# Second attention: a diagonal of softmax factors in place of the identity under three of four turned heads, and three buffers for turned tiles

## The chip, the cores and the metric

One core of a Trainium2 chip runs the whole program. The metric is its execution time in microseconds; times of the whole kernel are medians of runs. The profile is of one execution and is read by engine: PE (TensorE, matrix products and transposes through the array), DVE (VectorE), ACT (ScalarE), POOL (GpSimd) and SP, which issues most transfers.

## What is computed

The reference runs two transformer blocks one after the other on 512 tokens. The change lies in the attention of the second block. Each of its 16 query heads (two groups of eight, one key and value head for each group) attends in three ways: over 31 compressed blocks, over selected blocks (here all causal ones, since at most 8 of 16 picks exist) and over a window of 512. The three results are mixed by gates of each token and head:

```
s_c = einsum(qb, k_cmp) * scale;  p_c = masked_softmax(s_c, ...);  o_c = einsum(p_c, v_cmp)
s_s = einsum(qb, k_sel) * scale;  p_s = masked_softmax(s_s, ...);  o_s = einsum(p_s, v_sel)
s_w = einsum(qb, kwb)   * scale;  p_w = masked_softmax(s_w, ...);  o_w = einsum(p_w, vwb)
o = gb[..., 0:1] * o_c + gb[..., 1:2] * o_s + gb[..., 2:3] * o_w
```

So a row of exponentials must be multiplied by one factor: its gate divided by its sum.

## The kernel before

The tokens lie in four tiles of 128. For each of the two groups `g`, `queries(g)` makes the rotated queries, and then `attend(i, g, c, ...)` is called for each query tile `i` (0 to 3) and each `c` (0, 1), which stands for four heads: 16 calls. In a call, n = (i + 1) x 128 keys are seen.

In a call, PE forms scores of 128 queries by n keys for each of the four heads `a` and for two branches `br` (selected, window) into a PSUM bank (`s` or `sw`; L1439 and L1440, two products each); those with the compressed keys go along (`pc`). DVE adds the mask and takes the row's extreme (L1469). ACT takes the exponential and the row sum into `sm` (L1472). The compressed part `cs` goes through DVE, POOL and ACT by itself (L1476 to L1485). When all sums stand, DVE inverts them (L1482) and multiplies them by the gates (L1484); `sm[:, 1 + br, a]` is then the factor of a head and branch, one number for each query, and queries lie on partitions.

Then the exponentials are multiplied by their factors in place: heads 0 to 2 on DVE (L1493, six instructions of 128 x n), head 3 on ACT (L1491, two). After that PE turns them, so that keys lie on partitions: for each branch and each key tile `j` four transposes against the identity `ident` fill one PSUM bank `tp` (L1505), DVE (where j % 3 is 1) or ACT copies it to an SBUF tile `pT` of 128 x 512 (L1507), and two products with the values add it to the output bank `o` (L1510). Ahead of them the compressed part is turned (L1496), copied (L1498) and multiplied (L1500). At the end `split` makes the high and low part of `o` (`ynh`, `ynl`).

All operands of these transposes and of L1500 and L1510 are plain fp32. There are two `tp` banks, four `pT` buffers, three `s` banks, one `o` bank and 12 buffers for the exponentials. A scheduler lays out the order of the instructions on each engine when the program is built; it mixes in other products, those of the next group's queries and, in the second group, of the pooled branch (`mm`, L256, and `yp`, L1552). The attention runs from about 1905 to 2105 us of the span; behind it comes a long stretch of gated projections.

Of the kernel before, what the change touches and what calls it, by code (L numbers as in the profile page):

```python
# [9 lines left out]
F32 = mybir.dt.float32  # L10
# [3 lines left out]
AF = mybir.ActivationFunctionType  # L14
OP = mybir.AluOpType
AX = mybir.AxisListType

P = 128
T = 512
# [147 lines left out]
def build(tc, A, OUT):  # L167
    nc = tc.nc
    es = ExitStack()
    V, S, G, TE = nc.vector, nc.scalar, nc.gpsimd, nc.tensor  # L170
# [23 lines left out]
    def tpps(name="tp"):  # L194
        return bank(tp_tag[0], name)
# [7 lines left out]
    ident = cst[:, C_ID:C_ID + P]  # L203
# [35 lines left out]
    def wfm(name, c, kt=KD, width=P, c0=0):  # L239

        n = kt * width
        return kview(weights(A[name][c][:, c0:c0 + n], n, 2), kt, width)
# [218 lines left out]
    def mtwo(name="m2"):  # L461
        return tp.tile([P, L], F32, name=name, tag="m2", bufs=9)
# [66 lines left out]
    x = mtwo()  # L529
# [5 lines left out]
    pt = tpps(name="kpp")  # L535
    for t, t0, m in toks(L):
        TE.transpose(pt[:m, t * 32:(t + 1) * 32], x[:32, t0:t0 + m], ident[:32, :32])
    for t0, t1, m in ((0, NT, P), (NT, NT + 1, M)):
        h = t1 - t0
        pv = pt[:m, t0 * 32:t1 * 32].rearrange("p (t d) -> p t d", t=h)  # L540
        x = mtwo()
# [90 lines left out]
    def fm_pieces(w, pieces):  # L632

        x = two(t2)
        for a, b in pieces:
            ps = mmps()
            fm(ps[:, :b - a], w, hn, 0, a, b - a)
            S.copy(x[:, a:b], ps[:, :b - a])
        return x
# [110 lines left out]
    for h in range(8):  # L750
        x = fm_pieces(wfm("w_rv", h), PIECES)
        pt = tpps()
# [5 lines left out]
        pt = tpps()  # L758
# [102 lines left out]
    for c in range(KD):  # L861
        x = gate("w_za", c, two(t2)[:, :T])
# [45 lines left out]
    sts = ExitStack()  # L908
# [430 lines left out]
    for br in range(2):  # L1339
# [3 lines left out]
        r = rope_fm(ps)  # L1343
        o = (KS, KW)[br]
        for g in range(2):
            a, b = slice(g * 64, g * 64 + 64), slice(64 - g * 64, 128 - g * 64)
# [7 lines left out]
        x = two(t2)[:, :T]  # L1354
        S.copy(x, ps)
        pt = tpps()
# [10 lines left out]
    x = two(t2)[:48, :T]  # L1367
    S.activation(x, ps[:48], AF.Tanh, scale=0.5)
    V.tensor_scalar(x, x, 1.0, 0.5, op0=OP.add, op1=OP.mult)
    pt = tpps()  # L1370
# [11 lines left out]
    pt = tpps()  # L1382
# [12 lines left out]
    pt = tpps()  # L1395
# [11 lines left out]
    ap_ = pool("attn2", stack=sta)  # L1407
# [18 lines left out]
    def attend(i, g, c, Q, yh, yl):  # L1426

        n, t0 = (i + 1) * P, i * P
        cs = ap_.tile([P, 4, 32], F32, name="cs", bufs=2)
        mx = ap_.tile([P, 4, 2], F32, name="mx2", bufs=2)  # L1430
        sm = ap_.tile([P, 3, 4], F32, name="sm2", bufs=2)
        mc = ap_.tile([P, 4], F32, name="mc", bufs=2)
        mask = cst[:, C_MASK + (3 - i) * P:C_MASK + 512]
        cmask = cst2[:, K_CMP + i * 64:K_CMP + i * 64 + 32]
        sts = []

        def score(out, a, k0, m):
            q = Q[c][:, a, t0:t0 + P]
            TE.matmul(out, q, KH[:, g, k0:k0 + m], start=True, stop=False)  # L1439
            TE.matmul(out, q, KL[:, g, k0:k0 + m], start=False, stop=True)  # L1440

        if i == NT - 1:
            pc = bank("s", "pc")
            for a in range(4):
                score(pc[:, a * 32:a * 32 + 32], a, KC, 32)
            V.tensor_tensor(cs, pc[:, :P].rearrange("p (a k) -> p a k", a=4),
                            cmask[:, None, :].to_broadcast([P, 4, 32]), op=OP.add)
        for a in range(4):
            ps = bank("s", "s")
            if i == 0:  # L1450
                score(ps[:, :KS + P], a, K0, KS + P)
                src = (ps[:, KS:KS + P], ps[:, :P])
                pc = ps[:, KC:KC + 32]
            else:
                k0 = KS if i == NT - 1 else KC
                score(ps[:, :KS + n - k0], a, k0, KS + n - k0)
                pw = bank("s", "sw")
                score(pw[:, :n], a, KW, n)
                src = (ps[:, KS - k0:KS - k0 + n], pw[:, :n])
                pc = ps[:, :32]  # L1460
            if i < NT - 1:
                V.tensor_tensor(cs[:, a], pc, cmask, op=OP.add)
            s2 = []
            for br in range(2):
                if i < 2 and br:
                    s = s[:, n:]
                else:
                    s = ap_.tile([P, T], F32, name="s2", bufs=12)
                V.tensor_tensor_reduce(out=s[:, :n], in0=src[br], in1=mask, scale=-SC, scalar=3e38,  # L1469
                                       op0=OP.add, op1=OP.min, accum_out=mx[:, a, br:br + 1])  # L1470
                s2.append(s)
                S.activation(s[:, :n], s[:, :n], AF.Exp, scale=-1.0, bias=mx[:, a, br:br + 1],  # L1472
                             accum_out=sm[:, 1 + br, a:a + 1])
            sts.append(s2)

        V.tensor_reduce(mc, cs, axis=AX.X, op=OP.max)  # L1476
        G.tensor_tensor(cs, cs, mc[:, :, None].to_broadcast([P, 4, 32]), op=OP.subtract)
        S.activation(cs, cs, AF.Exp, scale=SC)
        V.tensor_reduce(sm[:, 0], cs, axis=AX.X, op=OP.add)
        G.tensor_tensor(cs, cs, cst2[:, None, K_CMP + i * 64 + 32:K_CMP + i * 64 + 64].to_broadcast([P, 4, 32]), op=OP.mult)  # L1480

        V.reciprocal(sm, sm)  # L1482
        h0 = 8 * g + 4 * c
        V.tensor_tensor(sm, sm, gv[:, i, :, h0:h0 + 4], op=OP.mult)  # L1484
        G.tensor_tensor(cs, cs, sm[:, 0, :, None].to_broadcast([P, 4, 32]), op=OP.mult)  # L1485
        for a in range(4):
            for br in range(2):
                s = sts[a][br][:, :n]
                r = sm[:, 1 + br, a:a + 1]
                if a == 3:  # L1490
                    S.activation(s, s, AF.Copy, scale=r)  # L1491
                else:
                    V.tensor_scalar(s, s, r, None, op0=OP.mult)  # L1493
        po = bank("o", "o")
        pt = tpps()
        TE.transpose(pt[:, :P], cs.rearrange("p a k -> p (a k)"), ident)  # L1496
        pT = ap_.tile([P, T], F32, name="pT", bufs=4)
        V.tensor_copy(pT[:, :P], pt[:, :P])  # L1498
        for j in range(2):
            TE.matmul(po[:, j * P:(j + 1) * P], vcb[:, g, j], pT[:, :P], start=j == 0, stop=False, skip_group_check=True)  # L1500
        for br in range(2):
            for j in range(i + 1):
                pt = tpps()
                for x, a in enumerate((0, 2, 1, 3)):
                    TE.transpose(pt[:, x * P:(x + 1) * P], sts[a][br][:, j * P:(j + 1) * P], ident)  # L1505
                pT = ap_.tile([P, T], F32, name="pT", bufs=4)
                (V.tensor_copy if j % 3 == 1 else S.copy)(pT, pt)  # L1507
                last = br == 1 and j == i
                for b in range(2):
                    TE.matmul(po[b * 64:b * 64 + 64, :2 * P], vt[:, j, br, g], pT[:, b * 256:b * 256 + 256],  # L1510
                              start=False, stop=last, skip_group_check=True)
        pv = po[:, :2 * P].rearrange("p (j t) -> p j t", j=2)
        split(pv, yh[:, 2 * c:2 * c + 2, t0:t0 + P], yl[:, 2 * c:2 * c + 2, t0:t0 + P])
# [46 lines left out]
    for c in range(KD):  # L1560
        y = gate("w_gm", KD + c, two(t2)[:, :T])
        gated("w_pn", c, ysl, KD, y)
        x = gate("w_gm", c, two(t2)[:, :T])
# [88 lines left out]
```

## Time and profile before

| what | us |
|---|---|
| median of 3 runs | 2685.57 (2683.2 to 2687.15) |
| the profiled execution | 2681.29 |
| its span | 2679.5 |
| PE busy in the span | 2585.8 |
| DVE busy in the span | 1702.9 |
| ACT busy in the span | 1146.1 |
| POOL busy in the span | 926.6 |

The span goes from the first to the last instruction of the profiled execution. Busy times of PE are modelled from pipelined instructions and overlap, so that a busy PE need not be working at its full pace; the pace is read from how many instructions of a kind pass in a given time in the chain of waits. In the trace an instruction keeps the line of the code that made it, and one matrix product in the code may be several instructions.

### The profile page before, as it was taken

The numbers are of one execution on the slowest core, as the hardware profiler recorded it, in microseconds if no ns is written. First come the engines' busy times: TensorE is split into PE (matmuls) and PEld (weight loads), VectorE is DVE, ScalarE is ACT, GpSimd is POOL, SyncE is SP. The second block draws the span as 40 slices with busy tenths as digits, with TensorE's granted clock in tenths as the row PEclk, the third lists the DMA queues.
The fourth block names the chain that finished last, engine by engine and source line by source line (L and its number), as shares of the span: only waits on it lengthen the run. The fifth ranks groups of instructions, "written<-read, shape, count | busy, mean of one in ns | idle before, by whom it ended". The sixth has DMA issues, their size and how long they took to land.

```text
span 2679.5 us, 37137 instructions
## 1 busy us (share of the span) xinstructions
PE 2585.8 (97%) x13809; PEld 2225.1 (83%) x13809; DVE 1702.9 (64%) x3399; ACT 1146.1 (43%) x2097; POOL 926.6 (35%) x590
## 2 busy tenths in 40 slices
PE   8899999999899999999999999999999999899998
PEld 7768778899899988888888888887666788787887
DVE  5772442246998992898989888866778412534333
ACT  5552342244577663333333333334667422422322
POOL 2122122325344342565555555522222233211112
PEclk9999999999999999999999999998999999999999
DMA  3322223323356568999999999963110122222221
GB/s 129 100 69 68 67 75 122 119 84 118 103 174 195 168 199 290 331 368 400 402 408 370 339 351 333 337 203 108 53 43 25 60 95 96 109 94 95 94 95 63
DMA packets 177957, 465.80 MB, mean 174 GB/s; under 512 B 15856, under 2 KB 78960, under 8 KB 171120
## 3 DMA queue, kind: packets, MB, share of 16 engines
q1 hardware_dynamic: 136736, 322.84, 34.7%
q0 software_dynamic: 36864, 134.23, 13.6%
q10 hardware_dynamic: 4176, 6.36, 0.8%
q8 instruction: 108, 1.77, 0.3%
q14 instruction: 73, 0.60, 0.1%
HBM read 421.17 MB, written 37.42 MB: 171 GB/s over the span
## 4 chain that ended last, share of the span: by engine, by line
PE 78%; DVE 14%; ACT 2%; DMA 2%; issue 2%; POOL 1%; ACTq 1%; SPq 0%; DVEq 0%; POOLq 0%
PE mm L256 36%; PE py L1182 19%; PE pu L256 13%; DVE oh L1093 3%; PE o L1510 2%; PE tp L1505 1%; DMA t<-t 1%; PE mm L1101 1%; DVE xn L350 1%; DVE oh L1065 1%; DVE oh L1068 1%; DVE oh L1096 1%; PE s L699 1%; DVE ef L1070 1%; DMA wr<-in_u_T_dram 1%
## 5 line engine op out<-in xcount | busy, mean ns | idle before, releaser
L211 POOL TENSOR_TENSOR wl<-wr,wh 128x1024 fp32r<-128x1024 f32 (+1 forms) x142 | 349.9, 2465 | 764.5 <-ACT wh L210 329.5
L210 ACT CAST wh<-wr 128x1024 fp32r<-128x1024 f32 (+2 forms) x271 | 273.4, 1010 | 311.2 <-PE mm L256 203.4
L256 PE MATMUL pu<-xf,wh 128*128 128x384 f32 x2048 | 392.3, 343 | 10.3 <-ACT wh L210 5.8
L256 PEld LDWEIGHTS pu<-xf,wh 128*128 128x128 f32 x2048 | 362.0, 190 | 16.3 <-ACT wh L210 6.2
L211 DVE TENSOR_TENSOR wl<-wr,wh 128x1024 fp32r<-128x1024 f32 (+2 forms) x129 | 152.0, 1179 | 184.0 <-ACT wh L210 112.2
L974 POOL DMA_INDIRECT row<-in_v_rows_dram,eg x128 | 195.7, 1529 | 163.7 <-DVE yg L989 136.9
L974 POOL DMA_INDIRECT row<-in_u_rows_dram,eg x128 | 187.8, 1467 | 176.2 <-DVE row L979 155.1
L256 PE MATMUL pu<-xf,wl 128*128 128x384 f32 x1024 | 202.4, 339 | 2.6 <-POOL wl L211 2.6
L1169 ACT CAST ah<-act 128x384 fp32r<-128x384 f32 x128 | 65.8, 514 | 324.0 <-DVE act L1166 302.2
L1182 PE MATMUL py<-vl,ah 128*128 128x512 f32 x768 | 195.8, 389 | 0.1
L1182 PE MATMUL py<-vh,ah 128*128 128x512 f32 x768 | 195.7, 389 | 0.0
L1182 PE MATMUL py<-vh,al 128*128 128x512 f32 x768 | 195.6, 389 | 0.0
L256 PEld LDWEIGHTS pu<-xf,wl 128*128 128x128 f32 x1024 | 182.5, 189 | 3.5 <-POOL wl L211 3.5
L1174 DVE TENSOR_TENSOR vl<-vr,vh 128x1024 fp32r<-128x1024 f32 x128 | 156.3, 1221 | 22.3 <-ACT vh L1172 22.3
L1182 PEld LDWEIGHTS py<-vl,ah 128*128 128x128 f32 x768 | 144.0, 188 | 30.6 <-DVE vl L1174 0.7
L1182 PEld LDWEIGHTS py<-vh,al 128*128 128x128 f32 x768 | 144.2, 188 | 30.0
L989 DVE SCALAR_TENSOR_TENSOR yg<-row,ag,yg 128x1024 f32<-128x1024 f32 x127 | 162.9, 1282 | 5.3 <-DMA row<-in_v_rows_dram,eg 2.9
L1182 PEld LDWEIGHTS py<-vh,ah 128*128 128x128 f32 x768 | 143.3, 188 | 25.4
L979 DVE SCALAR_TENSOR_TENSOR row<-row,xg 128x1024 f32<-128x1024 f32 x128 | 152.3, 1221 | 9.9 <-DMA row<-in_u_rows_dram,eg 9.9
L1093 DVE TENSOR_TENSOR oh<-iota,eT 128x1024 f32<-128x1024 f32 x96 | 139.8, 1483 | 14.0 <-PE mm L1101 12.6
L381 DVE TENSOR_TENSOR h<-mm,h 128x512 f32<-128x512 f32 (+1 forms) x54 | 34.1, 632 | 172.6 <-PE mm L256 172.6
L1172 ACT CAST vh<-vr 128x1024 fp32r<-128x1024 f32 x128 | 134.6, 1051 | 19.5 <-PE py L1182 18.7
(468 smaller groups left out, 5103.3 us busy)
## 6 DMA issues: line engine op xcount, KB each, us to landing
wr<-in_u_T_dram SPq DMA_DIRECT2D x128, 512.0 KB
vr<-in_v_rows_dram SPq DMA_DIRECT2D x128, 512.0 KB
wwr<-in_w_f_dram SPq DMA_DIRECT2D x32, 1024.0 KB
gates<-stg SPq DMA_DIRECT2D x24, 1024.0 KB
gin<-gates SPq DMA_DIRECT2D x16, 1536.0 KB
wr<-in_w_gm_dram SPq DMA_DIRECT2D x16, 512.0 KB
ahead<-act SPq DMA_DIRECT2D x41, 192.0 KB
act<-ahead SPq DMA_DIRECT2D x41, 192.0 KB
```

Of the source, the lines that this page charges most:

```text
L210: S.copy(hi, src)
L211: (lo_eng or V).tensor_tensor(lo, src, hi.bitcast(F32), op=OP.subtract)
L256: TE.matmul(out, w[a][k][:, c0:c0 + P], act[b][k][:, t0:t0 + n], start=i == 0 and k == 0, stop=i == 2 and k == kt - 1)
L974: G.indirect_dma_start(out=r, out_offset=None, in_=src, in_offset=bass.IndirectOffsetOnAxis(ap=eg[:, k:k + 1], axis=0))
L979: V.scalar_tensor_tensor(r, r, 1.0, xg, op0=OP.mult, op1=OP.mult, accum_out=ag[:, k:k + 1])
L989: V.scalar_tensor_tensor(yg[0], r, ag[:, k:k + 1], yg[0], op0=OP.mult, op1=OP.add)
L1093: V.tensor_tensor(a1, iota[:, None, None, :].to_broadcast([P, 2, 4, P]), eT[:, :2, b0 + q0:b0 + q0 + 4, None].to_broadcast([P, 2, 4, P]), ...
L1169: S.copy(ah, a)
L1172: S.copy(vh, raw)
L1174: V.tensor_tensor(vl, raw, vh.bitcast(F32), op=OP.subtract)
L1182: TE.matmul(py[2 * t + d], x[:, t * P:(t + 1) * P], w[:, d * 512:(d + 1) * 512], start=e == 0 and i == 0, stop=e == P - 1 and i == 2)
L1510: TE.matmul(po[b * 64:b * 64 + 64, :2 * P], vt[:, j, br, g], pT[:, b * 256:b * 256 + 256], start=False, stop=last, skip_group_check=True)
```

## The change

The multiplications of heads 0 to 2 are gone. Instead DVE makes for each branch a tile `dg` of 128 x 3 x 128 that holds three diagonal matrices: the identity times the factor of head 0, 1 and 2 of each query. Under these heads the transpose against the identity becomes an ordinary product against the diagonal, which turns and scales in one go. Head 3 is still scaled by ACT and turned by a transpose. `dg` has two buffers of 1.5 KB on each partition, one for each branch; `pT` has three buffers in place of four.

```diff
-        for a in range(4):
-            for br in range(2):
-                s = sts[a][br][:, :n]
-                r = sm[:, 1 + br, a:a + 1]
-                if a == 3:
-                    S.activation(s, s, AF.Copy, scale=r)
-                else:
-                    V.tensor_scalar(s, s, r, None, op0=OP.mult)
+        dg = [ap_.tile([P, 3, P], F32, name="dg", bufs=2) for br in range(2)]
+        for br in range(2):
+            V.tensor_tensor(dg[br], ident[:, None, :].to_broadcast([P, 3, P]),
+                            sm[:, 1 + br, :3, None].to_broadcast([P, 3, P]), op=OP.mult)
+            s = sts[3][br][:, :n]
+            S.activation(s, s, AF.Copy, scale=sm[:, 1 + br, 3:4])
...
-        pT = ap_.tile([P, T], F32, name="pT", bufs=4)
+        pT = ap_.tile([P, T], F32, name="pT", bufs=3)
...
                 for x, a in enumerate((0, 2, 1, 3)):
-                    TE.transpose(pt[:, x * P:(x + 1) * P], sts[a][br][:, j * P:(j + 1) * P], ident)
-                pT = ap_.tile([P, T], F32, name="pT", bufs=4)
+                    s = sts[a][br][:, j * P:(j + 1) * P]
+                    if a < 3:
+                        TE.matmul(pt[:, x * P:(x + 1) * P], s, dg[br][:, a], start=True, stop=True)
+                    else:
+                        TE.transpose(pt[:, x * P:(x + 1) * P], s, ident)
+                pT = ap_.tile([P, T], F32, name="pT", bufs=3)
```

The order of the instructions changes with it in the whole second attention. Two places show how, both in the first call with four key tiles of the second group (g = 1, i = 3, c = 0). On DVE before, the factors are followed by a score tile's minimum, by six scalings and by the copy of the turned compressed part:

```order
L1484 TENSOR_TENSOR sm_19029<-sm_19029,gts 128x12
L1469 ISA s_19218,mx_19187<-s,cstt 128x512
L1469 ISA mx_19187 128x1
L1493 TENSOR_SCALAR s_19047<-s_19047,sm_19029 128x512
L1493 TENSOR_SCALAR s_19050<-s_19050,sm_19029 128x512
L1493 TENSOR_SCALAR s_19059<-s_19059,sm_19029 128x512
L1493 TENSOR_SCALAR s_19062<-s_19062,sm_19029 128x512
L1493 TENSOR_SCALAR s_19071<-s_19071,sm_19029 128x512
L1493 TENSOR_SCALAR s_19074<-s_19074,sm_19029 128x512
L1498 COPY pT<-tp 128x128
```

On DVE now (lines behind the change have other numbers: the copy L1498 is L1497):

```order
L1484 TENSOR_TENSOR sm_19001<-sm_19001,gts 128x12
L1469 ISA s_19188,mx_19157<-s,cstt 128x512
L1469 ISA mx_19157 128x1
L1489 TENSOR_TENSOR dg<-cstt,sm_19001 128x384 x2
L1497 COPY pT<-tp 128x128
L1469 ISA s_19191,mx_19157<-sw,cstt 128x512
```

The two builds stand where the six scalings stood. On PE before, the first turned tiles of the same call have products of the pooled branch (L256) between them:

```order
L1505 MATMUL tp<-cstt,s_19047 128x128
L256 MATMUL mm<-h2h,wh 128x512 x6
L1505 MATMUL tp<-cstt,s_19071 128x128
L1505 MATMUL tp<-cstt,s_19059 128x128
L1505 MATMUL tp<-cstt,s_19083 128x128
L256 MATMUL mm<-h2h,wh 128x512 x2
L1500 MATMUL o<-pT,vcb 128x128 x2
L1510 MATMUL o<-pT,vt 64x256 x2
L1505 MATMUL tp<-cstt,s_19047 128x128
```

On PE now (L1506 is the product with the diagonal, L1508 the transpose, L1499 the former L1500, L1513 the former L1510):

```order
L1506 MATMUL tp<-dg,s_19019 128x128
L1506 MATMUL tp<-dg,s_19043 128x128
L1506 MATMUL tp<-dg,s_19031 128x128
L1499 MATMUL o<-pT,vcb 128x128 x2
L1508 MATMUL tp<-cstt,s_19055 128x128
L1506 MATMUL tp<-dg,s_19019 128x128
L1506 MATMUL tp<-dg,s_19043 128x128
```

The turning products now stand in closer rows, and the L256 products that lay between them have moved to other places, many of them behind the call.

## Rows read from the trace of the kernel before

**Rows 1.** The page: busy us, share of the span, instructions.
```profile
PE 2585.8 (97%) x13809; PEld 2225.1 (83%) x13809; DVE 1702.9 (64%) x3399; ACT 1146.1 (43%) x2097; POOL 926.6 (35%) x590
```

**Rows 2.** Busy times by stretch of the span, us: the attention and its four parts.
```profile
core 0: us, PE busy (x) PEld busy (x) DVE busy (x) ACT busy (x) POOL busy (x), PEclk, DMA share, GB/s
1905.00:2105.00 200.00, 190.57 (x1163) 130.66 (x1161) 157.70 (x550) 144.99 (x400) 43.09 (x67) 1.00 0.10 31
1911.00:1944.00 33.00, 29.16 (x186) 19.75 (x184) 29.10 (x135) 28.36 (x94) 6.41 (x13) 1.00 0.05 11
1944.00:2004.00 60.00, 56.94 (x352) 37.25 (x352) 42.86 (x108) 41.16 (x90) 11.95 (x13) 1.00 0.11 35
...
2014.00:2052.00 38.00, 36.42 (x221) 26.32 (x220) 34.64 (x138) 30.89 (x95) 12.68 (x19) 1.00 0.09 31
2052.00:2105.00 53.00, 52.82 (x337) 35.23 (x337) 37.96 (x110) 33.55 (x77) 7.10 (x15) 1.00 0.06 19
```

**Rows 3.** Chain of waits, 1905 to 2110: start us, us, what.
```profile
1949.36 0.59 PE tp L1505 x4
...
2057.35 1.01 PE o L1510 x8
2058.37 1.02 PE tp L1505 x8
...
2067.30 0.58 PE o L1510 x4
...
2079.91 1.39 PE mm L256 x6
...
2082.09 0.45 PE o L1500 x4
```

**Rows 4.** PE by line, 1905 to 2105: count, busy us, mean ns, idle before.
```profile
L1505 PE MATMUL tp<-cstt,s 128*128 128x128 f32 x320 | 51.9, 281 | 2.6 <-DVE s L1493 2.6
L1510 PE MATMUL o<-pT,vt 128*64 128x256 f32 x320 | 48.4, 400 | 0.4 <-DVE pT L1507 0.2
...
L256 PE MATMUL mm<-h2l,wh 128*128 128x512 f32 x64 | 21.0, 413 | 0.0
...
L1500 PE MATMUL o<-pT,vcb 128*128 128x128 f32 x64 | 10.2, 282 | 0.0
```

**Rows 5.** DVE by line and shape, 1905 to 2105: count, busy us, mean ns.
```profile
L1493 DVE TENSOR_SCALAR s<-s,sm 128x512 f32<-128x512 f32 x24 | 10.3, 495 | 0.0
L1493 DVE TENSOR_SCALAR s<-s,sm 128x384 f32<-128x384 f32 x24 | 8.5, 418 | 0.0
...
L1493 DVE TENSOR_SCALAR s<-s,sm 128x256 f32<-128x256 f32 x24 | 7.0, 357 | 0.0
...
L1493 DVE TENSOR_SCALAR s<-s,sm 128x128 f32<-128x128 f32 x24 | 5.6, 298 | 0.1
...
L1537 DVE TENSOR_TENSOR t<-t 128x511 f32<-128x511 f32 x4 | 2.7, 680 | 0.0
...
L1446 DVE TENSOR_TENSOR cs<-pc,cst 128x128 f32<-128x128 f32 x4 | 1.2, 292 | 3.7 <-PE pc L1440 3.7
```

**Rows 6.** Instructions in order of time in a call with four key tiles.
```profile
1989.13 2.55 DVE L1493 TENSOR_SCALAR s<-s,sm 128x512 f32<-128x512 f32 x6
...
1991.60 0.28 DVE L1498 COPY pT<-tp 128x128 f32<-128x128 f32 x1
```

**Rows 7.** Who waited for whom, 1905 to 2110: total us, times, longest us.
```profile
ACT pT L1507 <- PE tp L1505: 24.9, 28, 2.8
...
DVE pT L1507 <- PE tp L1505: 16.2, 16, 5.1
...
PEld o L1510 <- ACT pT L1507: 6.5, 24, 0.8
...
PEld tp L1505 <- DVE s L1493: 4.0, 6, 1.4
...
PE tp L1505 <- DVE s L1493: 2.6, 4, 1.1
```

## Prediction

> **What bounds the kernel now.** I read the page first: TensorE (PE) is busy 97% of the span, VectorE (DVE) 64% [rows 1]. That PE share is modelled, so it does not say how much PE could still take. Second I read the busy times by stretch, around the second attention, 1905 to 2105 us [rows 2]. The 16 calls of attend fall into four stretches: small query tiles of group 0 (i = 0, 1: 33 us), large ones (i = 2, 3: 60 us), and the same of group 1 (38 and 53 us). DVE is busy 88% and 91% in the two small stretches, 71% and 72% in the large ones. The granted clock is 1.00 in all four, so no gain or loss can come from the clock.
>
> How full PE really is comes from the pace of its instructions, read from the chain of waits [rows 3]: eight transposes take 1.02 us and four 0.59, so one more costs (1.02 - 0.59) / 4 = 0.108 us; the products into `o` give (1.01 - 0.58) / 4 = 0.108; four instructions of the 128x128 product at L1500 take 0.45, so 0.11; six 512-wide instructions of L256 take 1.39, so 0.232. The counts of 1905 to 2105 [rows 4] are 320 transposes (L1505), 320 instructions of L1510, 64 of L1500 and 191 of L256 (three rows of 64, 64 and 63). That leaves 1163 - 895 = 268 others, mostly score products of 256 to 512 columns, which I put midway between 0.11 and 0.23, at 0.17. Work: 35 + 35 + 7 + 44 + 46 = 167 us of 200. PE thus waits some 33 us here, and one instruction is 167 / 1163 = 0.143 us of work on average. By that mean the four stretches hold 26.6, 50.3, 31.6 and 48.2 us of PE work, and so 6.4, 9.7, 6.4 and 4.8 us of idle PE. So the small stretches are near DVE's limit, and the large ones near PE's.
>
> **The change part by part.**
>
> *Transposes become products.* Of the four heads three are multiplied by a diagonal. Which heads: 3 of 4 of 320, so 240. What a true product costs here is shown by L1500, which has the same 128x128 fp32 operands: the code issues 32 of them (2 in each of 16 calls) and the trace holds 64 instructions [rows 4], two for each product, at 0.11 us each [rows 3]; a transpose is one instruction of 0.108. So each of the 240 grows from 0.11 to 0.22 us: **240 x 0.11 = +26.4 us of PE work**: 4.0 us in each small stretch (36 products), 9.2 in each large one (84). The second weight load of each product I cost at nothing: L1500 has it too and still goes at 0.11 a piece; uncovered it would be inside that price.
>
> The Trainium skill speaks against this edit: "Perfetto Trace Analysis", section Transposes, asks that a logical transpose be a transpose and not a standard matmul, since transposes skip the arithmetic. By that rule PE work grows, without a figure. In "TensorE: Matmul & The Clock Gate", section Terms, the fp32 transpose mode is called four times faster; by that the added work would be an estimated 79 us instead of 26. The trace disagrees with the factor: two instructions against one, each at the same 0.11 [rows 3, 4].
>
> *The scalings go from DVE.* 96 TENSOR_SCALAR of 10.3 + 8.5 + 7.0 + 5.6 = 31.4 us leave [rows 5]. Instead 32 builds of a 128x384 diagonal come, a two-operand fp32 op that the trace has not at this size. Its neighbours: 0.29 us at 128 elements and 0.68 at 511 [rows 5]; between them 0.29 + 0.39 x 256 / 383 = 0.55 us. I take 0.55 (bounds 0.41, the price of a 128x384 scaling, and 0.68), so 32 x 0.55 = 17.6 us. **DVE is relieved of 13.8 us**, 3.5 in each small stretch (12 x 0.298 + 12 x 0.357 - 8 x 0.55), the other half in the large ones. The bounds give 18.3 and 9.6.
>
> *The hand-over in a call gets shorter.* Before, the six scalings stand in one run ahead of the copy L1498 on DVE, and PE waits for both: at 1989.1 the run takes 2.55 us and only then the copy starts [rows 6]. The new order has two builds there, 1.1 us, and then the copy. PE's own waits for the scalings, though, sum to only 2.6 + 4.0 us [rows 7], since other products fill most of the time. This is what DVE's relief can give at most directly: some 4 of these 6.6 us. It is part of the relief and not added to it.
>
> *A new wait.* The two diagonals are two buffers, so the builds of a call wait until the transposes of the call before are through; behind them on DVE stand the copy L1498, which PE waits for, and the row minima of the next call. In the new order all turning products of a call stand ahead of the next call's first use, so I put this at 0 (bounds 0 and one build in each call, 16 x 0.55 = 9 us). *Three pT buffers in place of four*: three are in flight in the new order (one of the compressed part and two), so 0; at most a wait of one pair of products, 0.43 us, in each call, 7 us. ScalarE (ACT) keeps its 32 scalings of the fourth head.
>
> **The sum.** A stretch takes PE's work and what idle PE is left. I let half of the idle remain, because part of it is waiting for a turned tile to be copied (25 us of ACT and 16 of DVE waiting for transposes, against 6.5 of PE waiting for ACT's copies [rows 7]): while PE does longer products, the copies of the tile before are hidden. The small stretch of group 0 then takes 26.6 + 4.0 + 3.2 = 33.8 us against 33, so +0.8; the large one 50.3 + 9.2 + 4.9 = 64.4 against 60, +4.4; the small one of group 1 31.6 + 4.0 + 3.2 = 38.8 against 38, +0.8; the large one 48.2 + 9.2 + 2.4 = 59.8 against 53, +6.8.
>
> That is +12.8. In the small stretches, where DVE is the later one, I grant half of its 3.5 us twice: -3.5. Sum **+9.3 us**. The profiled execution took 2681.3 us (span 2679.5), 4.3 below the median of 2685.6; so 2690.6 for such an execution, and 2685.6 + 9.3 = **2695 us** as the median. Ends: all idle taken up, 167 + 26.4 = 193.4 of 200, gives -6.6; none taken up, +26.4.
>
> **The rivals.**
>
> *DVE leads all through (faster).* If PE waits because DVE is late everywhere, the stretch follows DVE, and 13.8 us less there come off until PE itself is full. Place: the small stretches and the run of scalings. For it: 88% and 91% busy DVE [rows 2], the 2.55 us run [rows 6]. Against it: PE's 193 us of work set a floor 6.6 us below today's 200, and in the large stretches DVE idles 28%. It decides from the point where less than 0.5 us of idle PE is left. Price: 2685.6 - 6.6 = 2679 us.
>
> *Idle PE takes it all (no change).* Most of the 33 us of waits were for copies and for DVE, and the longer products lie in them. Then +26.4 is met by 20 to 30 us: within 5.4 us of today, about 2686. For it: the waits for copies [rows 7]. Against it: in the large stretches only 14.5 us of idle stand against 18.4 added.
>
> *Full price (slower still).* The idle does not shrink, because the filling products are laid out otherwise and the diagonals' buffers hold DVE: +26.4, 2712 us. For it: of the chain's own time the transposes are a large part already, and PE leads in the large stretches. Against it: DVE's relief and the copies that get hidden.
>
> *Four passes a product.* If a product with the diagonal took the time of four transposes, each would cost three more: 240 x 3 x 0.11 = 79 us, of which some 20 fall into idle PE, so 2685.6 + 59 = 2745. This is the factor of the page named above. Against it stands L1500, which takes two instructions for the same shapes and types [rows 4].
>
> **How the numbers follow.** 0.2% is 5.4 us, about what a measurement of this kernel can tell from no change. Forecast (+5.4 to +17): 0.50. Idle takes it all (within 5.4): 0.24. DVE leads: 0.13. Full price (+17 to +30): 0.10. Four passes: 0.03. So faster 0.13, same 0.24, slower 0.50 + 0.10 + 0.03 = 0.63. The range for 8 in 10 takes the forecast, the no-change case, and the near parts of the two neighbours: 2680 to 2711.
>
> **What would show it.** In the profile after: 560 instructions where 320 turned tiles before (480 with the diagonal, 80 transposes), at 0.11 us each in the chain; 32 builds of 0.41 to 0.68 us; DVE's busy time down by 10 to 18 us; the stretch from the first to the last turned tile about 9 us longer, almost all of it at i = 2 and 3, the small stretches about even; PE's waits for DVE's factors gone. I am wrong if a product with the diagonal takes one instruction, or one of 0.05 us; if the small stretches shorten by more than 3 us each; or if DVE waits for PE before the builds.

## The result and the profile after

The changed kernel is slower: 2713.6 us median (2711.63 to 2716.26, 4 runs) against 2684.78 for the kernel before on the same chip, a ratio of 1.0111 with a 95% interval of 1.0099 to 1.0123. That is **+28.8 us, where +9.3 was forecast**. The direction was right, the size three times too small, and 2713.6 lies above the range (2680 to 2711). The rival "full price" (2712 us), which had a chance of 0.10, has the right number; of its two reasons the runs bear out the filler that is laid out otherwise, but not the buffers of the diagonals.

In the changed kernel the copy L1498 is L1497, the former L1500 is L1499, the copy L1507 is L1510, the products L1510 are L1513, and the builds are L1489. First the busy times of the page of the kernel after (us, share of the span, instructions), beside [rows 1]:

```profile
PE 2623.1 (97%) x14049; PEld 2259.6 (83%) x14049; DVE 1691.2 (62%) x3335; ACT 1148.6 (42%) x2097; POOL 934.9 (34%) x590
```

PE has 240 instructions more, as forecast, and 37.3 us more of (modelled) busy time; DVE has 11.7 us less. The same view by stretch as [rows 2], cut at the calls of the kernel after: the whole attention, then small and large tiles of group 0, small and large tiles of group 1.

```profile
core 0: us, PE busy (x) PEld busy (x) DVE busy (x) ACT busy (x) POOL busy (x), PEclk, DMA share, GB/s
1905.00:2135.00 230.00, 224.42 (x1407) 163.35 (x1407) 146.50 (x487) 147.66 (x401) 46.88 (x67) 0.99 0.09 27
1911.00:1948.00 37.00, 34.70 (x225) 24.42 (x223) 29.58 (x123) 29.76 (x98) 7.09 (x14) 1.00 0.06 14
1948.00:2009.00 61.00, 60.60 (x400) 42.57 (x401) 30.81 (x83) 36.80 (x82) 9.04 (x11) 1.00 0.06 19
2028.00:2063.00 35.00, 34.75 (x232) 26.57 (x233) 30.69 (x118) 28.39 (x88) 9.83 (x16) 1.00 0.09 31
2063.00:2127.00 64.00, 62.15 (x408) 44.47 (x408) 32.21 (x88) 34.62 (x81) 8.33 (x13) 0.97 0.03 9
```

The granted clock is 1.00 in the first three parts and 0.97 in the last (0.83 from 2110 to 2120 us, which is worth 1.7 us of full clock and so little of the 28.8). DVE's share falls from 71 and 72% to 51 and 50% in the large stretches, and PE leads there by a wide margin. The operations themselves are as forecast (line, engine, operation, shapes, count, busy us, mean ns, idle before; answering [rows 4] and [rows 5]):

```profile
L1506 PE MATMUL tp<-dg,s 128*128 128x128 f32 x480 | 73.8, 287 | 0.1
L1508 PE MATMUL tp<-cstt,s 128*128 128x128 f32 x80 | 22.2, 277 | 0.0
L1489 DVE TENSOR_TENSOR dg<-cstt,sm 128x384 f32<-128x384 f32 x32 | 20.1, 663 | 0.2
```

Who waited for whom, 1905 to 2140, in total us, times and longest wait, answers [rows 7]:

```profile
ACT pT L1510 <- PE tp L1508: 37.9, 35, 3.1
DVE pT L1510 <- PE tp L1508: 31.6, 20, 5.8
...
PEld tp L1495 <- POOL cs L1485: 7.7, 10, 2.3
...
PEld o L1513 <- ACT pT L1510: 5.7, 24, 0.4
```

PE's waits for the scalings are gone, and its wait for ACT's copies is a little shorter (5.7 against 6.5). The two engines that copy turned tiles now wait 69.5 us for PE, where it was 41.1. Next to nothing waits on the new builds: PE's load queue waited for one of them 0.3 us, and DVE sat idle 0.2 us ahead of them. PE's wait for the compressed part, whose last step POOL does, has nothing to do with the change and stays (7.7 us above). Before it was:

```profile
PEld tp L1496 <- POOL cs L1485: 8.5, 11, 2.2
```

**Where the 28.8 us lie.** The spans of the two profiled executions are 31.7 us apart (2711.2 and 2679.5); 27.5 of them lie in the attention, as the table shows. The starts of the turned compressed part (L1496, now L1495) mark the calls, and the last products of a group mark its end. Filler is the products of L256, for the next queries and for the pooled branch.

| stretch | before, us | after, us | filler before | filler after |
|---|---|---|---|---|
| small tiles, group 0 | 33.1 | 36.8 | 5 | 5 |
| large tiles, group 0 | 59.1 | 60.7 | 48 | 22 |
| from group 0 to group 1 | 11.1 | 19.3 | 33 | 64 |
| small tiles, group 1 | 37.7 | 34.9 | 45 | 23 |
| large tiles, group 1 | 53.4 | 64.0 | 35 | 25 |
| from the last call to the next product with ynh | 1.9 | 8.1 | 7 | 34 |
| sum | 196.3 | 223.8 | 173 | 173 |

The calls are 13.1 us longer. That this is near the forecast's 9.3 is chance, since it counted no filler as leaving them. The other 14.4 us stand in the two stretches between calls, of which the forecast said nothing: 58 filler instructions have left the calls, and 58 x 0.232 = 13.5 us. The filler's rows alone (windows of L256 only: PE busy us and instructions; a window cut at a whole us can count a few of its neighbour's) show it, first before, then after:

```profile
1944.00:2003.00 59.00, 15.09 (x48) 8.61 (x48) 1.00 0.12 35
2003.00:2014.00 11.00, 8.41 (x33) 5.93 (x33) 1.00 0.26 74
```

```profile
1948.00:2009.00 61.00, 7.06 (x22) 4.30 (x23) 1.00 0.06 19
2009.00:2028.00 19.00, 15.90 (x65) 11.56 (x63) 1.00 0.30 84
```

**How much PE really waited before.** The chain of waits of the kernel before runs for long stretches through PE alone, each piece starting where the last one ends (start us, us, what):

```profile
1950.12 0.58 PE o L1510 x4
1950.71 0.59 PE tp L1505 x4
1951.29 0.18 PE sw L1440
1951.47 0.58 PE o L1510 x4
1952.05 0.59 PE tp L1505 x4
1952.64 0.58 PE o L1510 x4
1953.22 0.21 PE pc L1439
```

There is no wait here, and yet four products into `o` take 0.58 us, and not 4 x 0.108 = 0.43. In the whole attention before, each of the 44 rows of four takes 0.582 us or more (median 0.583) from its start to the next instruction, and each of the 18 rows of eight 1.015: 43.9 us for the 320, where the forecast counted 35. From the last of them to what follows it is 0.309 to 0.310 us, nearly always, whether a turning, a score product or a filler stands next. So 0.15 us is a fixed cost of such a row, not a wait. The same holds for a row of four turnings between such rows (0.59 us). The forecast took the difference of rows of four and of eight as the pace, and called the fixed part idle.

Counted anew, from start to start with every instruction at the pace of its kind (0.109 us for a turning, 0.108 for a product into `o`, 0.23 for 512 columns, and so on), PE stands still for over 0.12 us at 28 places before, 14.0 us in all. After it is 27 places and 10.4 us. Smaller gaps, which are mostly the fixed costs, went from 24.1 to 31.7 us, and work from 158.2 to 181.6 (26 of products, less 2.6 for six products of the pooled branch that moved behind). These sums shift by some us with the paces that are taken, their differences by about 1 us. So the waits shrank by 3.5 us, and the small gaps took 7.6 more. Nor need the 3.5 us be the products' doing: in the kernel with the builds and without the products (below) the waits shrink at least as much, to 9.8 us. And of the 14.0 us, 6.1 stood ahead of the turned compressed part, for which POOL is late, where a longer turning does not reach.

### The profile page after: what moved, and what is told of

Read it like the earlier page. It is cut to its first block, busy times and chain, and to the rows that moved or that the text cites. A ratio compares the mean times of both kernels' runs of the same rounds, so it can differ in the third digit from the quotient of the medians.

```text
span 2711.2 us, 37556 instructions
## 1 busy us (share of the span) xinstructions
PE 2623.1 (97%) x14049; PEld 2259.6 (83%) x14049; DVE 1691.2 (62%) x3335; ACT 1148.6 (42%) x2097; POOL 934.9 (34%) x590
## 5 line engine op out<-in xcount | busy, mean ns | idle before, releaser
L256 PE MATMUL pu<-xf,wh 128*128 128x384 f32 x2048 | 391.0, 342 | 10.3 <-ACT wh L210 5.4
L256 PEld LDWEIGHTS pu<-xf,wh 128*128 128x128 f32 x2048 | 360.9, 190 | 16.5 <-ACT act L961 5.8
L256 PE MATMUL pu<-xf,wl 128*128 128x384 f32 x1024 | 201.2, 338 | 2.6 <-POOL wl L211 2.6
L256 PEld LDWEIGHTS pu<-xf,wl 128*128 128x128 f32 x1024 | 181.4, 188 | 3.5 <-POOL wl L211 3.5
L211 POOL TENSOR_TENSOR wwl<-wwr,wwh 128x2048 fp32r<-128x2048 f32 x11 | 51.7, 4702 | 263.4 <-ACT wwh L210 263.4
```

The source lines that it names most:

```text
L211: (lo_eng or V).tensor_tensor(lo, src, hi.bitcast(F32), op=OP.subtract)
L256: TE.matmul(out, w[a][k][:, c0:c0 + P], act[b][k][:, t0:t0 + n], start=i == 0 and k == 0, stop=i == 2 and k == kt - 1)
```

## The experiments

The first theory: an added turning product is paid in full, since it stands on the chain from turning to copy to product, with PE the latest link. Rivals: the builds or the buffers hold the kernel, the two `tp` banks do, or the order in which filler is laid out.

**The products alone.** The scalings stay, and the three heads are turned by products with the plain identity.

```diff
-                    TE.transpose(pt[:, x * P:(x + 1) * P], s, ident)
+                    if a < 3:
+                        TE.matmul(pt[:, x * P:(x + 1) * P], s, ident, start=True, stop=True)
+                    else:
+                        TE.transpose(pt[:, x * P:(x + 1) * P], s, ident)
```

> The scalings stay on VectorE and pT keeps four buffers, but heads 0 to 2 are turned by an ordinary product against the identity: the 240 longer turnings alone. Full price (a turning product holds up all that follows on TensorE, none of it falls into idle time): +24 to +28 us over the kernel before. Half absorbed, as I forecast: +11 to +15 us. If the +29 of the changed kernel comes from the builds, their two buffers or the third pT buffer: under +10 us.

Measured: 2711.66 us, 1.0105 (1.0086 to 1.0124), +27.8 us. The products alone bring the whole loss: 27.8 / 240 = 0.116 us for each added instruction. Here only one filler instruction stands between the groups (33 before, 64 in the change), so the loss does not hang on that move of the filler.

**The scalings taken out.** Heads 0 to 2 are left unscaled, with nothing in the scalings' place, so DVE has 31.4 us less to do and PE the same.

```diff
                 if a == 3:
                     S.activation(s, s, AF.Copy, scale=r)
-                else:
-                    V.tensor_scalar(s, s, r, None, op0=OP.mult)
```

> Heads 0 to 2 are not scaled at all (the output leaves their factors out), nothing is built, transposes as before: the whole relief of VectorE, 31 us of its work, alone. Full price, with TensorE leading: -1 to -7 us. VectorE leading: -14 us or more. If PE's idle is copy turn-around and not VectorE's load: within 4 us of no change.

Measured: 2678.87 us, 0.9978 (0.9969 to 0.9987), -5.0 us. All of the scalings are worth a sixth of their time. PE's waits of over 0.12 us fall by about as much, from 14.0 to 9.2 us.

**The builds alone.** The diagonals are made as in the change, and nothing reads them: heads 0 to 2 are turned unscaled by transposes, with three pT buffers.

```diff
-                    if a < 3:
-                        TE.matmul(pt[:, x * P:(x + 1) * P], s, dg[br][:, a], start=True, stop=True)
-                    else:
-                        TE.transpose(pt[:, x * P:(x + 1) * P], s, ident)
+                    TE.transpose(pt[:, x * P:(x + 1) * P], s, ident)
```

> VectorE's side of the change alone: heads 0 to 2 not scaled, the 32 builds made but not used, three pT buffers, all turnings transposes (the output leaves the factors out). Without the builds the relief gave -5 us. If it is worth what it takes off VectorE (11 of 31 us): -1 to -3 us. If the builds stand in the way of the copies and minima behind them: +2 us or more.

Measured: 2679.01 us, 0.9984 (0.9975 to 0.9993), -4.1 us. That is more than the -1 to -3 us expected, though the interval reaches them. 20 us of builds cost about 1 us against none at all, within the intervals. In the code this kernel differs from the change only in the kind of the 240 turnings (the order is laid out anew for it), and the change stands 32.9 us above it.

**Three pT buffers** in the kernel before:

```diff
-                pT = ap_.tile([P, T], F32, name="pT", bufs=4)
+                pT = ap_.tile([P, T], F32, name="pT", bufs=3)
```

> The kernel before with three pT buffers, nothing else. If the third buffer is harmless, as I forecast: within 3 us of no change. If it is what kept idle TensorE from being filled: +5 to +15 us.

Measured: 2684.03 us, 1.0004 (0.9995 to 1.0013): nothing.

**A third and twice the products.** In the first kernel only head 0 is turned by a product (80 instructions added, about 8.8 us; the scalings stay). In the second each product with a diagonal is made twice (480 more than in the change, about 53 us; the second overwrites the first with the same).

```diff
-                    if a < 3:
+                    if a < 1:
```

> The scalings stay on VectorE, four pT buffers, and head 0 alone is turned by an ordinary product: 80 added instructions, 8.8 us of TensorE, a third of the 240 that gave +27.8. Full price from the first product on: +8 to +10 us. If idle takes up the first ones and only the later ones are paid: within 4 us of no change.

```diff
+                        TE.matmul(pt[:, x * P:(x + 1) * P], s, dg[br][:, a], start=True, stop=True)
                         TE.matmul(pt[:, x * P:(x + 1) * P], s, dg[br][:, a], start=True, stop=True)
```

> The changed kernel with each product against the diagonal done twice, the second over the first: 480 more instructions at 0.11 us, 53 us of TensorE. Full price: +50 to +56 us over the changed kernel. If idle is still being taken up at this load: +40 or less.

Measured: one head 2691.83 us, 1.0028 (1.0016 to 1.004), +7.0 us, 0.088 for each added instruction; twice 2769.07 us, 1.0311 (1.0297 to 1.0326), 55.5 us above the change, 0.116 each. There is no dose that the idle time takes up: the first 8.8 us already cost 7.0, a little under the 8 to 10 expected, with an interval from 4.3 to 10.7. The chain of waits of the doubled kernel, between 2097 and 2110 us, is PE alone:

```profile
by line: PE tp L1506 33.7%; PE tp L1507 29.2%; PE o L1514 22.3%; PE tp L1509 5.3%; PE o L1499 3.4%; PE tp L1495 2.6%; PE mm L256 1.8%; PE sw L1440 1.4%; PE sw L1439 1.3%
```

**Three tp banks.** One score bank is given to the turned tiles, in the change and, as a control, in the kernel before.

```diff
-    psum("s", 3, st)
-    psum("tp", 2, st)
+    psum("s", 2, st)
+    psum("tp", 3, st)
```

> The changed kernel with three PSUM banks for turned tiles and two for scores, in place of two and three. If TensorE's idle is the turn-around of the two banks (turn, copy, turn again): -8 us or more against the changed kernel, 2705 or less. If a score bank is as dear as a turning bank: within 4 us of it, or slower.

> The kernel before with the same exchange of one bank, as a control. Turn-around of two banks: -5 us or more. Score banks as dear: no change or slower by up to 10 us.

Measured: the change with three banks 2717.49 us, 1.0132 (1.0116 to 1.0147), +34.3 us over the kernel before, where the change is at +28.8; the control 2689.75 us, 1.0018 (1.0009 to 1.0027), +6.6 us. The exchange costs the change 5.5 us and the kernel before 6.6. What a third tp bank gives by itself is not separated from what the missing score bank takes, but it gives the change no more than it gives the kernel before, so the two tp banks are not what makes the products dear.

**The products in one instruction.** Exponentials and diagonals are rounded when written (low bits of the fp32 are lost), and a turning product then takes one instruction, as a transpose does (240 in the traces, where the change has 480). The first of two kernels has separate buffers for the fourth head (9 and 3), the second keeps 12 in common and has the order of the change row for row.

```diff
-                    s = ap_.tile([P, T], F32, name="s2", bufs=12)
+                    s = ap_.tile([P, T], F32R, name="s2", bufs=12)
...
-        dg = [ap_.tile([P, 3, P], F32, name="dg", bufs=2) for br in range(2)]
+        dg = [ap_.tile([P, 3, P], F32R, name="dg", bufs=2) for br in range(2)]
```

> The changed kernel with diagonal and exponentials of heads 0 to 2 held in the rounded fp32 type that TensorE takes in one instruction (scores and exponentials of these heads lose low bits; their twelve buffers are split into nine and three): 240 instructions less, the rest of the change stays. Full price: the +29 goes almost wholly, between -6 and +4 us against the kernel before. If builds, buffers or order are to blame: +15 us or more remain.

> The changed kernel with the exponentials of all heads and the diagonals in the rounded fp32 type, the twelve buffers shared as before (the run with nine and three had 19 us left, which the split of the buffers may have cost). The order on every engine is that of the changed kernel, row by row; only the 240 products take one instruction in place of two (scores, exponentials and factors lose low bits). Full price by the second instruction: -24 to -29 us against the changed kernel, so -2 to +5 against the kernel before. If the new order, the builds or the two diagonal buffers carry the loss: +10 us or more against the kernel before.

Measured: 2702.74 us, 1.007 (1.0055 to 1.0085), +18.8 us over the kernel before, and 2697.35 us, 1.0048 (1.0034 to 1.0061), +14.2 us. The case "full price", that the second instruction is the whole loss, missed in both, and both meet the sign that was set for order, builds or buffers. The second is 14.6 us below the change: half of the loss comes back when the second instruction of the products goes, and the other half stays, with as many PE instructions as in the kernel before. The builds, with the same buffers, cost next to nothing above. What the second kernel's trace shows is PE waiting for the copy of a turned tile (1905 to 2130 us; 5.7 us in the change and 6.5 before):

```profile
PEld o L1513 <- ACT pT L1510: 13.5, 34, 1.0
```

Its waits of over 0.12 us are 24.9 us at 76 places, with the 20 us at a low clock that follow left out, where the kernel before has 14.0 and the change 10.4. Ahead of the products into `o` they are 14.3 us (2.4 before, 1.8 in the change). So in the order of the change, which the scheduler laid out for the longer turnings, the copies are hidden while PE does two instructions, as the forecast argued, and come late when it does one. The builds alone, with the same number of PE instructions in an order of their own, have 9.8 us of waits and are 18.3 us faster. Whether the order or the rounded type makes this difference, no run separates.

In the profiled execution the granted clock also fell to its lower level, 1.2 GHz (windows of 10 us; the clock, as a share of 2.4 GHz, stands before the last two columns):

```profile
1940.00:1950.00 10.00, 8.83 (x39) 5.27 (x39) 9.11 (x37) 9.53 (x28) 2.28 (x5) 0.92 0.08 20
1950.00:1960.00 10.00, 10.00 (x38) 5.24 (x38) 5.88 (x12) 5.75 (x13) 5.23 (x3) 0.50 0.32 105
1960.00:1970.00 10.00, 10.00 (x39) 7.90 (x38) 6.35 (x19) 4.57 (x11) 0.40 (x1) 0.56 0.01 2
```

The call that holds most of these 20 us took 19.0 us (1947.1 to 1966.1), in the change 13.2. But this execution is the longest of the kernel's five (2704.07 us, mean clock 0.982). The one at the median, 2697.35 us, had a mean clock of 0.987, as the kernel before, so the fall does not explain the +14.2 us. The filler lies as in the change, 22 instructions in the large tiles of group 0 and 64 between the groups.

**Filler cut.** The projection of the pooled branch (L256, through `fm` in the loop on `w_u`) is made with 2 of 24 instructions in each of four groups, so 88 are left out, 20.4 us of PE time off the chain.

```diff
-        fm(ps, w, hn, 0, 0, T)
+        TE.matmul(ps, w[0][0][:, :P], hn[0][0][:, :T], start=True, stop=False)
+        TE.matmul(ps, w[1][0][:, :P], hn[1][0][:, :T], start=False, stop=True)
```

> The kernel before with the projections of the pooled branch cut from 24 instructions of 512 columns to 2 each (88 fewer, 20.4 us of TensorE; their result is then not the reference's): the second group's attention loses the products that a scheduler laid between its calls. If these products only filled idle time: 0 to -8 us. If TensorE leads there: -15 to -20 us.

> The changed kernel with the same cut. Against the kernel before with the cut: if the added products met no idle because the filling products already lay in it, the difference falls from +29 to +24 or less, as half of the attention has idle to give now. If the idle lies in turn-arounds that each added product only pushes back, it stays at +26 to +30.

Measured: in the kernel before 2680.97 us, 0.9988 (0.9979 to 0.9997), -3.9 us for 20.4 us of work; in the change 2706.26 us, 1.0072 (1.0059 to 1.0086), 7.3 us below the change. So most of this filler lay in waits, and perhaps less of it does so in the change (each interval reaches some 3 us to either side). The waits appear when it goes: PE's places over 0.12 us rise from 14.0 to 28.2 us in the kernel before, and PE's load queue waits longer for the factors (1905 to 2110, where it was 4.0 us, [rows 7]):

```profile
PEld tp L1505 <- DVE s L1493: 7.7, 10, 1.4
```

The difference that the change makes, with the filler cut in both, is still 25.3 us. It lies between the two cases that were set (24 or less, 26 to 30) and does not decide between them; but most of the price is there without this filler.

**Filler added.** In the kernel before the same projection is made twice: 96 instructions more, 22.3 us.

```diff
         fm(ps, w, hn, 0, 0, T)
+        fm(ps, w, hn, 0, 0, T)
```

> The kernel before, with the projection of the pooled branch that fills in between the second group's turnings computed twice: the same products once more, 96 instructions of 512 columns, 96 x 0.232 = +22.3 us of TensorE work off the chain of turn, copy and product. Theory that added work is paid only on the chain: filler lies in the waits, +4 to +12 us against before (taking 20.4 us of the same filler away was worth 3.9). Rival, that TensorE is full here and pays for everything: +20 to +24 us.

Measured: 2706.67 us, 1.0085 (1.0071 to 1.0099), +23.5 us by the medians. The chain theory's number (+4 to +12) falls, and the rival's (+20 to +24) holds. The chain shows where the added work went. The large tiles of group 1 take 1 us more than before, and then (start us, us, what):

```profile
2102.68 0.58 PE o L1510 x4
2103.26 23.84 PE mm L256 x103
```

All of it stands bare behind the last call; in the kernel before 7 instructions stood there. The order laid none of it into the waits, which are 13.8 us as against 14.0. So the theory must be widened: it is not only the chain's products that are paid in full here, but any work that the order puts where PE has no wait. That PE is full, as the rival has it, is not shown by this run: whether another order could have laid the added work into the waits is not tested. Cutting is another matter: what goes leaves waits in its place, so that 20.4 us of filler gave 3.9 and 31.4 us of scalings 5.0.

**Time taken off the chain.** In the kernel before turned tiles and values are rounded when written, and the products of a turned tile with the values become one instruction of 512 columns in place of four of 256. The compressed part takes four products in place of two, and the split at a call's end is made in two halves.

```diff
-                for b in range(2):
-                    TE.matmul(po[b * 64:b * 64 + 64, :2 * P], vt[:, j, br, g], pT[:, b * 256:b * 256 + 256],
-                              start=False, stop=last, skip_group_check=True)
-        pv = po[:, :2 * P].rearrange("p (j t) -> p j t", j=2)
-        split(pv, yh[:, 2 * c:2 * c + 2, t0:t0 + P], yl[:, 2 * c:2 * c + 2, t0:t0 + P])
+                TE.matmul(po[:64], vt[:, j, br, g], pT, start=False, stop=last, skip_group_check=True)
+        for b in range(2):
+            pv = po[:64, b * 2 * P:(b + 1) * 2 * P].rearrange("p (j t) -> p j t", j=2)
+            x = slice(b * 64, b * 64 + 64)
+            split(pv, yh[x, 2 * c:2 * c + 2, t0:t0 + P], yl[x, 2 * c:2 * c + 2, t0:t0 + P])
```

> The kernel before, but the turned tiles and the values are rounded on being written (the low bits of their fp32 are left out), and the products of a turned tile with the values are one instruction of 512 columns in place of four of 256 columns at 0.108 us: 0.232 against 0.43 us for each of 80 turned tiles, -16 us of TensorE work on the chain; the compressed part takes four instruction pairs in place of two, +3.5 us, and the split of a call is in two halves, about 16 x 0.8 us more on VectorE and ScalarE, off the chain. Theory that the chain is paid in full: -9 to -15 us against before. Rival, that the waits for copies set the pace and not TensorE's work: within 4 us of before. If the granted clock falls in the one-instruction stretch, as it did in e8_one_pass12, up to 10 us of the gain goes.

Measured: 2672.2 us, 0.9959 (0.9945 to 0.9973), **-11.0 us: faster than both kernels**, at the cost of some low bits. The chain shows the products at their new price, and eight turnings behind wide products at 0.87 us, where they took 1.02 behind the pairs [rows 3]:

```profile
1956.69 0.38 PE o L1510
1957.08 0.87 PE tp L1506 x8
...
1959.02 0.47 PE o L1510 x2
1959.48 0.87 PE tp L1506 x8
```

From a wide product to the next turning it is 0.285 us (median of 54), 0.05 over its pace of 0.23, where a row of four paired products has 0.15 over. So most of the fixed cost goes with the pairs. More filler lies in the calls: 73 instructions in the large tiles of group 0, and none between the groups. From the first call to the next product with `ynh` it is 195 in place of 173, so that 22 fewer, 5.1 us, are left for the stretch behind it. In the profiled execution the granted clock was at 0.50 for 13.6 us of this stretch, in three pieces.

**Both.** The rounded diagonals of the second one-instruction kernel (e8_one_pass12) on top of that kernel, so that DVE loses 31.4 us of scalings for 20.1 of builds while PE's work stays.

> e8_one_pass12 and e13_pv_one_pass together: exponentials, diagonals, turned tiles and values are all rounded on being written, the turning products take one instruction as the transposes do, and the products with the values one of 512 columns in place of four. TensorE's work is that of e13_pv_one_pass; VectorE loses 31.4 us of scalings and gets 20.1 us of builds. Theory that TensorE is full in the kernel before and that e13's cut (-11.0) left it waiting for VectorE and GpSimd: some of the 11 us come off, 2 to 6 us under e13, 2666 to 2670 us. Rival, that one-instruction turnings bring the granted clock down as in e8_one_pass12 (+16 over its like with transposes): 2678 to 2690 us.

Measured: 2683.78 us, 0.9997 (0.9988 to 1.0006): the gain of 11 us is gone. The time is the rival's, but not by its mechanism, since the granted clock in the profiled execution is 1.00 in every window of 10 us from 1900 to 2120. What the trace shows is the filler outside the calls once more: 27 instructions in the large tiles of group 0 against 73, and 59 between the groups against none (windows of L256 as above):

```profile
1949.00:1999.00 50.00, 7.50 (x26) 5.01 (x26) 1.00 0.08 24
1999.00:2017.00 18.00, 15.27 (x62) 10.99 (x60) 1.00 0.30 87
```

PE's waits of over 0.12 us are 32.0 us in it, against 21.3 in the kernel without the diagonals. Of these, 18.0 stand ahead of the products into `o`, against 1.5: PE waits for copies of turned tiles again (in the kernel without the diagonals the same line has 2.8 us, 12 times):

```profile
PEld o L1513 <- ACT pT L1511: 15.6, 30, 1.9
```

So the relief of DVE was worth less than what PE now waits for copies. The pattern, little filler in the large tiles of group 0, comes in each kernel without the scalings of the three heads (7 to 27 instructions against 48 before), but also in one that keeps them (27 with the products alone). What in the ordering makes it is open.

## Why the prediction was wrong

*The step that failed is the sum: "half of the idle remains".* It failed twice. First the idle itself, 33 us, was too large. The pace was taken from differences between rows of four and of eight in [rows 3], and the fixed 0.15 us that each of these rows also holds was dropped; so switches between kinds of products were called idle. Waits of over 0.12 us were 14.0 us, less than half of the 33, and 6.1 of them were for the compressed part. Second, half of the idle of the four stretches, 13.6 us, was to absorb products, and the waits shrank by 3.5 us, no more than with DVE's relief alone. With 23.5 us of work added, 7.6 more in short gaps and 3.5 back from the waits, the sum is 27.6; the attention grew by 27.5 us, and the kernel by 28.8. That longer products hide copies is true in a fixed order (the one-instruction products there save only 14.6 of some 26 us), but the kernel before had no such copies to hide: ahead of its products into `o` PE waited for 2.4 us. The point against "full price", that DVE's relief and hidden copies would pay part of it, was worth 4 to 5 us in the runs without products, and in the change it is not to be seen beside the small gaps.

*The stretches.* Small tiles were to stay about even, and together they did (+0.9), but by +3.7 and -2.8; large ones were to grow by 11.2 (4.4 and 6.8) and grew by 12.2 (1.6 and 10.6). That the sums agree is chance, since the forecast had no filler leave the calls. The step left out the two stretches between calls, where +14.4 us came from 58 filler instructions that moved. The order printed ahead of the prediction said that they had moved behind the call; their price, 13.5 us, was not put into the sum. It comes to the same thing as the idle: inside the calls 13.5 us of filler left and 26.4 us of products came, and the calls are 13.1 us longer. Nothing was absorbed there.

*Transposes become products*: right. 480 + 80 instructions; in the chain of waits of the kernel after, six products in a row take 0.67, so 0.112 each:

```profile
2066.21 0.58 PE o L1513 x4
2066.79 0.42 PE tp L1506 x2
2067.21 0.58 PE o L1513 x4
2067.79 0.64 PE tp L1506 x4
...
2068.54 0.67 PE tp L1506 x6
2069.21 0.11 PE tp L1508
```

This is PE alone, too: between 2062 and 2085 us the chain has no piece of another engine. The rule on transposes that the prediction weighed (the Trainium skill, "Perfetto Trace Analysis", section Transposes) was borne out by the time: 27.8 us for 240 of them. A product took the time of two transposes, so the factor of four, and with it the rival "four passes", did not come.

*DVE's relief*: right in kind, its size off. A build takes 0.66 us, near the upper bound, so 20.1 us of builds and a relief of 11.3 in place of 13.8 us; the page has 11.7. Its worth, taken as 3.5 us in the sum, was 4.1 us in the run on it alone, and 5.0 where all the scalings went.

*The new wait and the three buffers*: right at 0. PE's load queue waited 0.3 us for a build, and three pT buffers made no difference.

*DVE leads all through*: refuted. With all 31.4 us of scalings gone the kernel gained 5.0 us. *Idle takes it all*: refuted at every dose tried (80, 240 and 720 added instructions).

## What to carry to other kernels

Before idle time is promised to new work, take the length of whole rows from the chain, start to next start: what a row costs beyond its pace was here a price of changing between kinds of products, and it took in nothing. Where filler already lies in the waits, as here, expect PE work that is added on the chain to cost its full time even if other engines are relieved, and put what it pushes out into the sum where it lands. Shortening PE's own rows (one wide product in place of four paired ones) gave 11.0 us here, and relief of DVE at most 5.0. The two did not add up: with both, PE waited for copies.

## What the runs showed of the chip beyond that

- The next instruction after a row of paired products (two outputs of 64 partitions) starts 0.309 to 0.310 us after the last one starts, in each of the 62 rows of the kernel before, whether it is a turning, a score product or filler. A row of four takes 0.583 us and a row of eight 1.015.
- The granted clock fell to 0.50 at 1948.4 us and stayed there for 20 us in the profiled execution of the kernel with one-instruction turnings. In the 10 us up to 1948 PE was 88% busy at a clock of 1.00. The five executions of this kernel had mean clocks from 0.982 to 0.987, and the later kernel with the same turnings was profiled at 1.00 throughout the attention, so the fall does not come with the turnings each time. What sets it off is not settled here.
